# Attention on one core: row statistics of the two key sets meet by copies between partition quarters on GpSimd instead of a trip through DRAM, and q's band copy is made some steps later

## The chip, the cores and the metric

The kernel runs on one core of a Trainium2 chip. The metric is the device time of one execution in microseconds, and the median of several executions counts. On a core, TensorE (PE in the profile; its weight loads are PEld), VectorE (DVE), ScalarE (ACT), GpSimd (POOL) and SyncE (SP) each work through a queue of their own, in order. They wait for each other and for DMAs through semaphores. In this kernel SyncE issues all DMAs.

## The reference

One layer of an encoder is computed for 256 prompt tokens and 1024 sample tokens, all in float32: a feed-forward block, a mixer, a second feed-forward block, with norms around each. The mixer is dilated attention (8 heads of 64) beside a depthwise convolution. Each query attends in three dilated branches, and the branches are merged by their softmax denominators:

```python
DILATED_BRANCHES = ((128, 1), (512, 4), (2048, 16))
def dilated_attention(q, k, v):
    ...
    for window, dilation in DILATED_BRANCHES:
        o, lse = dilated_branch(q, k, v, slopes, dilation, window // (2 * dilation))
        ...
    w = jax.nn.softmax(jnp.stack(lses), axis=0)
    o = jnp.sum(w[..., None] * jnp.stack(outs), axis=0)
```

## The kernel before

The program runs its stages one after the other: feed-forward 1, the projections to q, k, v with the convolution, the attention, the output projection, feed-forward 2. Products are made of a rounded and a rest part, in three passes of TensorE (lines 198 to 200). The change touches only the attention (`attn`, line 774).

**Two key sets.** The three branches of a sample token are computed as two sets of keys. Tokens lie by residue: token 4i + c is row i of residue c. Set A holds the keys of the same residue (256 of them), set B the near keys of all residues. For set A the 256 rows of a residue are two units of 128 partitions, so a head has units 0 to 7. For set B the queries are taken in 8 bands of 128 (32 rows of each of the 4 residues), units 10 to 17, from a reordered copy `qb` of q. Units 8 and 9 are the prompt. Two units make a group, so a head has nine groups, 0 to 8.

**Statistics.** For each unit, DVE adds the bias to the scores and keeps the row minimum (line 855), and ACT takes the exponential and keeps the row sum (line 861). Both go to `st`, 128 partitions by 36 columns: column 2u is the minimum of unit u, 2u + 1 its sum. A token has one pair from set A and one from set B, in different partitions: with row i = 32 (4h + r) + j, set A has it in partition 32r + j, set B in partition 32c + j. To scale the two outputs to one softmax, the pairs must meet. This is the merge.

**The merge before.** `merge1` (line 874) transposes `st` on PE, copies it out on ACT, stores it to DRAM (`sd`) and loads it back as four pieces into `az`, where both sets stand in one order. `merge2` takes the common minimum on DVE, `merge3` the exponentials on ACT, `merge4` forms the two factors on DVE, stores them to DRAM (`fd`) and loads them broadcast over 64 partitions (`F`, the tile x in the profile). `combine1` (line 1005) multiplies the two outputs by the factors on GpSimd, for two heads at a time, and `combine2` adds them (GpSimd and DVE).

**Other work that the change touches.** `load_qk` loads q and k of the head after next into one of two sets of buffers, and before the change also makes `qb` on GpSimd (line 803). `next_tab` halves the bias tables for the next head, `tab[0]` on DVE after group 4 and `tab[1]` on GpSimd after group 8 (line 822); groups 5 to 8 of the next head read `tab[1]`.

**Order.** The code walks over 72 steps (8 heads by 9 groups): scores of this step's group, transposes of the group four steps back, products with v six steps back. `when(k, g, f)` calls f(h) k steps after group g of head h:

```python
            when(2, 8, merge1)
            when(7, 8, merge3)
            ...
            when(6, 8, merge2)
            when(8, 8, merge4)
            when(13, 8, combine2)
            ...
            when(10, 8, combine1)
```

This is not yet the order on the engines. A scheduler takes the instructions of the whole program and lays down each engine's queue by times of its own, so an instruction can stand some places earlier or later than the code has it. The order on each engine is then fixed.

Of the kernel before, what the change touches and what calls it, by code (L numbers as in the profile page):

```python
# [10 lines left out]
F32 = mybir.dt.float32  # L11
F32R = mybir.dt.float32r
AF = mybir.ActivationFunctionType
OP = mybir.AluOpType
# [3 lines left out]
P = 128  # L18
# [4 lines left out]
NS = 1024  # L23
# [5 lines left out]
NH = 8  # L29
# [119 lines left out]
class Trunk:  # L149
# [624 lines left out]
    def attn(self, qk, pool, rpool, qd, kd, vd, after):  # L774
        nc = self.nc
        mm = nc.tensor.matmul
        H = {}

        KW = 288
        bufs = []  # L780
        for i in range(2):
            q = qk[i].tile([P, NT], F32R, name=f"q{i}")
# [12 lines left out]
        def load_qk(h):  # L795
            d = H.setdefault(h, {})
            q, qb, k, d["v"] = bufs[h % 2]
            f = slice(h * HD, (h + 1) * HD)
            for i in range(2):
                nc.sync.dma_start(q[i * HD:(i + 1) * HD].bitcast(F32), qd[i, f, :])  # L800
            for z, o, s in ((0, 0, 0), (0, HD, 0), (1, 0, 1), (1, HD, 1)):
                nc.sync.dma_start(k[z][o:o + HD, :, 16:16 + 256].bitcast(F32), kd[s, f, :].rearrange("f (c i) -> f c i", c=5))
            nc.gpsimd.tensor_copy(qb.rearrange("p (b c j) -> p b c j", b=8, c=4),
                                  q[:, 0:NS].rearrange("p (c b j) -> p b c j", b=8, c=4).bitcast(F32))
            d["q"], d["qb"], d["k"] = q, qb, k

        def load_v(h):
            o = h % 2 * HD
# [62 lines left out]
                nc.vector.tensor_scalar(d["P"][u], d["P"][u], d["st"][:, 2 * u + 1:2 * u + 2], None, op0=OP.mult)  # L871


        def merge1(h):
            d = H[h]
            st = d["st"]
            ps = self.bank("psm")
            nc.tensor.transpose(ps[:36, :P], st, self.ident)
            sb = pool.tile([36, P], F32, name="asb", tag="asb", bufs=2)
            nc.scalar.activation(sb, ps[:36, :P], AF.Copy)  # L880
            sd = self.dp.tile([36, P], F32, name=f"sd{h}")
            nc.sync.dma_start(sd, sb)
            z = pool.tile([32, 4, 32], F32, name="az", tag="az", bufs=2)
            for i in range(2):
                nc.sync.dma_start(z[:, i, :], sd[0:16, :].rearrange("(c h s) (r j) -> s c h r j", h=2, s=2, j=32)[i])
                nc.sync.dma_start(z[:, 2 + i, :], sd[20:36, :].rearrange("(b s) (c j) -> s c b j", s=2, j=32)[i])
            d["z"] = z

        def merge2(h):
            d = H[h]  # L890
            z = d["z"]
            y = pool.tile([32, 4, 32], F32, name="ay", tag="ay", bufs=2)
            v = nc.vector
            v.tensor_tensor(y[:, 3, :], z[:, 0, :], z[:, 2, :], op=OP.min)
            for i in range(2):
                v.tensor_tensor(y[:, i, :], y[:, 3, :], z[:, 2 * i, :], op=OP.subtract)
            d["y"] = y

        def merge3(h):
            nc.scalar.activation(H[h]["y"][:, 0:2, :], H[h]["y"][:, 0:2, :], AF.Exp)  # L900

        def merge4(h):
            d = H[h]
            y, z, v = d["y"], d["z"], nc.vector
            for i in range(2):
                v.tensor_tensor(z[:, 2 * i + 1, :], z[:, 2 * i + 1, :], y[:, i, :], op=OP.mult)
            v.tensor_tensor(y[:, 3, :], z[:, 1, :], z[:, 3, :], op=OP.add)
            v.reciprocal(y[:, 2, :], y[:, 3, :])
            for i in range(2):
                v.tensor_tensor(y[:, i, :], y[:, i, :], y[:, 2, :], op=OP.mult)  # L910
            fd = self.dp.tile([2, NS], F32, name=f"fd{h}")
# [112 lines left out]
        load_v(0)  # L1024
        load_qk(1)
        load_v(1)

        def at(i):
# [279 lines left out]
```

## Time and profile before

| | us |
|---|---|
| median of 3 runs | 2394.32 |
| lowest, highest | 2393.75, 2397.75 |
| the profiled execution | 2392.03 |
| its span in the trace | 2390.2 |

The page gives busy time by engine for the whole span. The attention is a short part of it, from about 1203 us (first score instruction) to about 1390 us, so what matters is read from the same views limited to that stretch. Idle time of an engine counts where PE idles with it.

### The profile page before, as it was taken

To read this page: it belongs to the slowest core of one execution; us is meant where nothing else is said; L and a number is where in the kernel's file an instruction comes from. 1 tells how busy PE (TensorE), PEld (TensorE's weight loads), DVE (VectorE), ACT (ScalarE), POOL (GpSimd) and SP (SyncE) were. 2 spreads that over 40 slices of the span, in tenths; PEclk is the share of its full clock that TensorE was granted. 3 is DMA by queue.
4 is the path that set the end of the run, shared out by engine and by line. 5 is a ranking of instruction groups with operands and counts; after the bars stand their busy time and mean duration, and the time that the engine had idled before them with its cause. 6 is when DMAs were issued, how large, how long until landed. Compare 5 with 4: busy or idle time off the path is not lost.

```text
span 2390.2 us, 30540 instructions
## 1 busy us (share of the span) xinstructions
PE 2298.5 (96%) x11788; PEld 1965.1 (82%) x11788; DVE 1269.1 (53%) x1796; ACT 810.6 (34%) x1530; POOL 643.1 (27%) x574
## 2 busy tenths in 40 slices
PE   7999999999999999999978889999999999999996
PEld 6888888888788887888877778888888888788885
DVE  5743444434545576996355643743444434545557
ACT  4322222223212134654366632322222222312123
POOL 2332322321000044985112333222323223000004
PEclk9999999999999999999988999999999999999998
DMA  4212212124222343322286542212122122422224
GB/s 156 64 62 69 74 59 81 63 69 146 93 84 81 99 130 111 113 80 75 92 167 139 124 151 89 73 58 82 62 69 75 58 82 73 144 90 84 93 79 152
DMA packets 210840, 223.79 MB, mean 94 GB/s; under 512 B 32324, under 2 KB 162660, under 8 KB 210694
## 3 DMA queue, kind: packets, MB, share of 16 engines
q1 hardware_dynamic: 210694, 221.84, 30.7%
q8 instruction: 92, 1.51, 0.3%
q14 instruction: 54, 0.44, 0.1%
HBM read 163.65 MB, written 58.15 MB: 93 GB/s over the span
## 4 chain that ended last, share of the span: by engine, by line
PE 85%; DMA 5%; DVE 3%; issue 2%; ACT 2%; POOL 1%; SPq 1%; POOLq 0%; ACTq 0%; DVEq 0%
PE psAB L198 8%; PE psAB L199 8%; PE psAB L200 8%; PE psd L198 7%; PE psd L199 7%; PE psd L200 7%; PE psR L199 3%; PE psR L200 3%; PE psR L198 3%; PE psC L198 3%; PE psC L199 3%; PE psC L200 3%; PE psgu L198 2%; PE psgu L199 2%; PE psgu L200 2%
## 5 line engine op out<-in xcount | busy, mean ns | idle before, releaser
L115 DVE TENSOR_TENSOR wb<-raw,wb 128x512 fp32r<-128x512 f32 x240 | 167.2, 698 | 217.5 <-ACT wb L114 212.8
L114 ACT ACTIVATE wb<-raw 128x512 fp32r<-128x512 f32 x240 | 150.8, 629 | 329.2 <-PE psAB L200 138.4
L207 POOL TENSOR_SCALAR st<-st 128x1 f32<-128x1 f32 x70 | 40.8, 583 | 634.0 <-ACT tmp L206 361.1
L198 PE MATMUL psd<-wd,ahl 128*128 128x512 f32 x500 | 196.6, 393 | 8.9 <-ACT y L563 3.8
L199 PE MATMUL psd<-wd,ahl 128*128 128x512 f32 x500 | 194.7, 389 | 0.0
L200 PE MATMUL psd<-wd,ahl 128*128 128x512 f32 x500 | 194.7, 389 | 0.0
L452 POOL TENSOR_TENSOR ac<-ac,tmp 128x512 f32<-128x512 f32 x40 | 67.5, 1688 | 468.4 <-DVE tmp L448 445.3
L534 ACT ACTIVATE ahl<-ar 128x512 fp32r<-128x512 f32 (+1 forms) x132 | 73.0, 557 | 350.4 <-PE psd L200 251.9
L199 PE MATMUL psR<-hT2l,wb 128*128 128x256 f32 x640 | 181.1, 283 | 0.0
L200 PE MATMUL psR<-hT2h,wb 128*128 128x256 f32 x640 | 180.9, 283 | 0.0
L198 PE MATMUL psR<-hT2h,wb 128*128 128x256 f32 x640 | 180.5, 282 | 0.0
L198 PEld LDWEIGHTS psR<-hT2h,wb 128*128 128x128 f32 x640 | 122.2, 191 | 6.1
L199 PEld LDWEIGHTS psR<-hT2l,wb 128*128 128x128 f32 x640 | 122.2, 191 | 4.7
L198 PE MATMUL psAB<-hT0h,wb 128*128 128x512 f32 x320 | 125.7, 393 | 0.0
L198 PE MATMUL psC<-hT1h,wb 128*128 128x512 f32 x320 | 125.5, 392 | 0.0
L199 PE MATMUL psAB<-hT0l,wb 128*128 128x512 f32 x320 | 125.4, 392 | 0.0
L114 ACT ACTIVATE wb<-g 128x512 fp32r<-128x512 f32 x80 | 50.6, 632 | 220.8 <-POOL g L136 96.5
L199 PE MATMUL psC<-hT1l,wb 128*128 128x512 f32 x320 | 125.4, 392 | 0.0
L200 PE MATMUL psAB<-hT0h,wb 128*128 128x512 f32 x320 | 124.5, 389 | 0.0
L200 PE MATMUL psC<-hT1h,wb 128*128 128x512 f32 x320 | 124.5, 389 | 0.0
L200 PEld LDWEIGHTS psR<-hT2h,wb 128*128 128x128 f32 x640 | 122.2, 191 | 1.6
L565 DVE TENSOR_TENSOR y<-y,psd 128x1024 f32<-128x1024 f32 x70 | 85.3, 1218 | 71.2 <-PE psd L200 71.2
(385 smaller groups left out, 6263.3 us busy)
## 6 DMA issues: line engine op xcount, KB each, us to landing
raw<-in_ffn_w_gu_dram SPq DMA_DIRECT2D x88, 512.0 KB
ad<-ac SPq DMA_DIRECT2D x88, 256.0 KB
g<-in_ffn_w_down_dram SPq DMA_DIRECT2D x44, 512.0 KB
ar<-ad SPq DMA_DIRECT2D x88, 256.0 KB
raw<-in_w_in_dram SPq DMA_DIRECT2D x20, 512.0 KB
ar<-ad SPq DMA_DIRECT2D x44, 128.0 KB
ad<-x SPq DMA_DIRECT2D x40, 128.0 KB
x2d<-y SPq DMA_DIRECT2D x10, 512.0 KB
```

Of the source, the lines that this page charges most:

```text
L114: nc.scalar.activation(out[:, 0], src, AF.Copy)
L115: nc.vector.tensor_tensor(out[:, 1], src, out[:, 0].bitcast(F32), op=OP.subtract)
L198: mm(out, lh[0], rh[0], start=first, stop=False, skip_group_check=more)
L199: mm(out, lh[0], rh[1], start=False, stop=False, skip_group_check=more)
L200: mm(out, lh[1], rh[0], start=False, stop=last, skip_group_check=more)
L207: nc.gpsimd.tensor_scalar(st[:, 0:1], st[:, 0:1], 1e-6 / (mul * mul), None, op0=OP.add)
L452: nc.gpsimd.tensor_tensor(a1, a1, q, op=OP.mult)
L534: nc.scalar.activation(hl[0], r, AF.Copy)
L565: nc.vector.tensor_tensor(y[b], y[b], o, op=OP.add)
```

## The change

The first part of the merge no longer goes through DRAM. `merge1` is now 16 small copies on GpSimd: for each residue c and each quarter r, 32 partitions of set A's statistics go from partitions 32r to 32r + 31 to partitions 32c to 32c + 31, into a tile X that is laid out as set B's statistics are. `merge2` to `merge4` compute on 128 partitions by 8 columns instead of 32 by 32. The transpose on PE and the copy on ACT move behind the factors (`merge5`), where 16 columns are transposed instead of 36; the factors are then stored to `fd` by two DMAs and loaded broadcast as before. The steps of the merge are called at other distances. The copy `qb` of the head after next is called eight steps after group 8 instead of with the loads, and at the start for heads 0 and 1.

```diff
@@ load_qk
-            nc.gpsimd.tensor_copy(qb.rearrange("p (b c j) -> p b c j", b=8, c=4),
-                                  q[:, 0:NS].rearrange("p (c b j) -> p b c j", b=8, c=4).bitcast(F32))
+        def cast_qb(h):
+            q, qb = bufs[h % 2][0:2]
+            nc.gpsimd.tensor_copy(qb.rearrange("p (b c j) -> p b c j", b=8, c=4),
+                                  q[:, 0:NS].rearrange("p (c b j) -> p b c j", b=8, c=4).bitcast(F32))
@@ merge1
-            nc.tensor.transpose(ps[:36, :P], st, self.ident)
...
-            nc.sync.dma_start(sd, sb)
...
-                nc.sync.dma_start(z[:, i, :], sd[0:16, :].rearrange("(c h s) (r j) -> s c h r j", h=2, s=2, j=32)[i])
-                nc.sync.dma_start(z[:, 2 + i, :], sd[20:36, :].rearrange("(b s) (c j) -> s c b j", s=2, j=32)[i])
+            d["X"] = pool.tile([P, 8, 2], F32, name="ax", tag="ax", bufs=2)
+            x = d["X"].rearrange("p (h r) s -> p h r s", h=2)
+            for c in range(4):
+                for r in range(4):
+                    nc.gpsimd.tensor_copy(x[c * 32:(c + 1) * 32, :, r, :],
+                                          d["st"][r * 32:(r + 1) * 32, 4 * c:4 * c + 4].rearrange("p (h s) -> p h s", s=2))
@@ merge2
-            v.tensor_tensor(y[:, 3, :], z[:, 0, :], z[:, 2, :], op=OP.min)
+            v(y[:, 3], d["X"][:, :, 0], z[:, :, 0], op=OP.min)
...
@@ merge4, merge5
-            nc.sync.dma_start(fd.rearrange("s (p j) -> p s j", j=32), y[:, 0:2, :])
+        def merge5(h):
+            ps = self.bank("psm")
+            nc.tensor.transpose(ps[:16, :P], d["y"].rearrange("p i b -> p (i b)")[:, 0:16], self.ident)
+            sb = pool.tile([16, P], F32, name="asb", tag="asb", bufs=2)
+            nc.scalar.activation(sb, ps[:16, :P], AF.Copy)
+            for i in range(2):
+                nc.sync.dma_start(fd[i].rearrange("(c b j) -> b c j", c=4, b=8), sb[8 * i:8 * i + 8].rearrange("b (c j) -> b c j", c=4))
@@ the steps
-            when(2, 8, merge1)
-            when(7, 8, merge3)
+            when(5, 8, merge5)
+            when(3, 8, merge3)
...
-            when(6, 8, merge2)
-            when(8, 8, merge4)
+            when(1, 8, merge1)
+            when(2, 8, merge2)
+            when(4, 8, merge4)
+            when(8, 8, lambda h: cast_qb(h + 2) if h + 2 < NH else None)
```

Up to the attention the queues are the same. In it, three places show what the change moves. Lines of the changed kernel are some numbers higher: the score instruction is 858, the q copy 807, the table 825, the first product of `combine1` 1013.

DVE, merge of head 1, before: it stands behind the scores of group 3 of head 2 (L855 is a score instruction, L894 and L896 are `merge2`, `az` is loaded from DRAM).

```order
L855 ISA pr,ast<-pss,g 128x256
L855 ISA ast 128x1
L894 TENSOR_TENSOR ay<-az 32x32
L896 TENSOR_TENSOR ay<-ay,az 32x32 x2
L855 ISA pr,ast<-pss,g 128x256
L855 ISA ast 128x1
L855 ISA pr,ast<-pss,g 128x256
L855 ISA ast 128x1
L924 COPY pT<-pst 128x512
```

DVE, merge of head 1, now: L892 to L894 are `merge2`, `ax` is the tile that GpSimd's copies fill, `ast` holds the statistics.

```order
L858 ISA pr,ast<-pss,g 128x256
L858 ISA ast 128x1
L929 COPY pT<-pst 128x512
L892 TENSOR_TENSOR ay<-ax,ast 128x8
L893 TENSOR_TENSOR ay<-ay,ax 128x8
L894 TENSOR_TENSOR ay<-ay,ast 128x8
L858 ISA pr,ast<-pss,g 128x256
L858 ISA ast 128x1
L858 ISA pr,ast<-pss,g 128x256
L858 ISA ast 128x1
L902 TENSOR_TENSOR ay<-ax,ay 128x8
```

The merge stands right behind the scores of group 8 of its own head, four groups earlier, and it waits for GpSimd where it waited for a DMA.

POOL before, from the q copy for head 3 on: L803 is the q copy, L822 the table, L1008 and L1017 are `combine1` and `combine2` of heads 0 and 1.

```order
L803 CAST qb1_9269<-q1_9268 128x1024
L822 TENSOR_SCALAR g_9279<-g_9279 128x768
L803 CAST qb0_9259<-q0_9258 128x1024
L822 TENSOR_SCALAR g_9279<-g_9279 128x768
L1008 TENSOR_TENSOR to_9707<-to_9707,x_9653 128x1024
L1008 TENSOR_TENSOR to_9706<-to_9706,x_9654 128x1024
L1017 TENSOR_TENSOR hT0h_9218<-to_9706,to_9707 128x512
L1017 TENSOR_TENSOR hT1h_9220<-to_9706,to_9707 128x512
L803 CAST qb1_9269<-q1_9268 128x1024
```

POOL now, from the table after head 1 to the copies of head 3: L884 are the 16 copies, `ax_9954` is head 2's and `ax_10200` head 3's.

```order
L825 TENSOR_SCALAR g_9279<-g_9279 128x768
L807 CAST qb1_9269<-q1_9268 128x1024
L884 COPY ax_9954<-ast_9705 32x2x2 x16
L1013 TENSOR_TENSOR to_9734<-to_9734,x_9585 128x1024
L1013 TENSOR_TENSOR to_9733<-to_9733,x_9586 128x1024
L825 TENSOR_SCALAR g_9279<-g_9279 128x768
L807 CAST qb0_9259<-q0_9258 128x1024
L1022 TENSOR_TENSOR hT0h_9218<-to_9733,to_9734 128x512
L1022 TENSOR_TENSOR hT1h_9220<-to_9733,to_9734 128x512
L884 COPY ax_10200<-ast_9945 32x2x2 x16
```

Each head's 16 copies have come into the queue. The products of heads 0 and 1 (L1013) now stand ahead of the table after head 2 and of the q copy for head 4, where they stood behind both.

SP before, merge of head 2: L882 and L885, L886 are the trip through `sd`, L912 stores `fd`; L800, L802, L812 and L814 load q, k and v.

```order
L882 DMA sd2_9950<-asb_9948 36x128
L812 DMA v0_9262<-vd_88 128x2x64
L885 DMA az_9952<-sd2_9950 32x1x32
L886 DMA az_9952<-sd2_9950 32x1x32
L885 DMA az_9952<-sd2_9950 32x1x32
L886 DMA az_9952<-sd2_9950 32x1x32
L800 DMA q1_9268<-qd_86 64x1280 x2
L814 DMA v0_9262<-vd_88 32x9x64 x4
L812 DMA v1_9272<-vd_88 128x2x64 x3
L802 DMA kH1_9270<-kd_87 64x5x256 x2
L912 DMA fd2_10115<-ay_10054 32x2x32
L802 DMA kL1_9271<-kd_87 64x5x256 x2
```

SP now, merge of head 2: L917 stores `fd` in two DMAs, L924 loads it broadcast; L800, L802, L815 and L817 load q, k and v.

```order
L817 DMA v0_9262<-vd_88 32x9x64
L917 DMA fd2_10068<-asb_10066 8x4x32 x2
L817 DMA v0_9262<-vd_88 32x9x64
L924 DMA x_10071<-fd2_10068 64x1024
L924 DMA x_10072<-fd2_10068 64x1024
L817 DMA v0_9262<-vd_88 32x9x64 x2
L800 DMA q1_9268<-qd_86 64x1280 x2
L815 DMA v1_9272<-vd_88 128x2x64 x4
L802 DMA kH1_9270<-kd_87 64x5x256 x2
```

The five DMAs through `sd` and `az` are gone; the store of the factors is two DMAs, and the loads of q for head 5 stand behind the broadcast loads.

## Rows read from the trace of the kernel before

**Rows 1.** The page of the profiled execution: its span, and part 1, the busy time of each engine with its share of the span and its instructions.

```profile
span 2390.2 us, 30540 instructions
...
PE 2298.5 (96%) x11788; PEld 1965.1 (82%) x11788; DVE 1269.1 (53%) x1796; ACT 810.6 (34%) x1530; POOL 643.1 (27%) x574
```

**Rows 2.** Stretches of the span, five of the attention: the stretch in us, its length, then busy time and count of instructions of PE, PEld, DVE, ACT and POOL, the granted TensorE clock (1.00 is full), the busy share of the DMA engines and GB/s.

```profile
1240.00:1376.00 136.00, 113.06 (x675) 100.43 (x675) 76.63 (x331) 86.04 (x278) 38.47 (x22) 0.88 0.62 132
1262.00:1274.00 12.00, 11.86 (x85) 10.84 (x84) 6.28 (x27) 8.53 (x30) 9.57 (x6) 1.00 0.87 174
1274.00:1279.30 5.30, 1.16 (x9) 0.91 (x8) 1.33 (x8) 0.99 (x4) 0.78 (x1) 0.91 0.09 14
1279.30:1286.00 6.70, 6.70 (x26) 5.90 (x27) 5.68 (x21) 3.87 (x14) 0.00 (x0) 0.56 0.75 153
1286.00:1298.00 12.00, 11.48 (x82) 10.30 (x81) 6.97 (x30) 9.19 (x31) 3.14 (x2) 1.00 0.87 178
```

**Rows 3.** Who waited for whom between 1200 and 1410 us, all engines: total us, times, longest us.

```profile
DVE ay L894 <- DMA az<-sd: 37.3, 8, 5.8
...
PE pst L930 <- DVE ast L855: 20.2, 6, 4.4
```

**Rows 4.** The chain that ended last, between 1265 and 1282 us, in order of time: start us, us, what. SPq is the queue of SyncE, which issues the DMAs.

```profile
1268.26 6.86 DMA sd<-asb
...
1275.14 0.73 SPq L885
...
1275.92 1.92 DMA az<-sd
...
1279.27 1.08 PE pst L930 x4
```

**Rows 5.** Timeline of DVE, start us, us, what (in brackets the idle time before it and what ended it). L855 is the score instruction, two to a group, nine groups to a head: the first of head 1; of group 7 of head 2 and group 3 of head 3; of group 7 of head 3 and group 3 of head 4; of head 7, and of its groups 3 and 7, with the merge between these two.

```profile
1219.39 0.42 DVE L855 CUSTOM_DVE_ANT_0 pr<-pss,g 128x256 f32<-128x256 f32 x1 [2.26 <-PE pss L851]
...
1262.21 0.43 DVE L855 CUSTOM_DVE_ANT_0 pr<-pss,g 128x256 f32<-128x256 f32 x1 [2.24 <-PE pss L851]
...
1271.62 0.42 DVE L855 CUSTOM_DVE_ANT_0 pr<-pss,g 128x256 f32<-128x256 f32 x1
...
1285.88 0.42 DVE L855 CUSTOM_DVE_ANT_0 pr<-pss,g 128x256 f32<-128x256 f32 x1 [1.01 <-PE pss L851]
...
1295.91 0.42 DVE L855 CUSTOM_DVE_ANT_0 pr<-pss,g 128x256 f32<-128x256 f32 x1
...
1357.73 0.42 DVE L855 CUSTOM_DVE_ANT_0 pr<-pss,g 128x256 f32<-128x256 f32 x1 [0.61 <-PE pss L851]
...
1363.70 0.42 DVE L855 CUSTOM_DVE_ANT_0 pr<-pss,g 128x256 f32<-128x256 f32 x1
...
1366.35 0.18 DVE L894 TENSOR_TENSOR ay<-az 32x32 f32<-32x32 f32 x1 [1.86 <-DMA az<-sd]
...
1373.00 0.35 DVE L855 CUSTOM_DVE_ANT_0 pr<-pss,g 128x256 f32<-128x256 f32 x1
```

**Rows 6.** Timelines of DVE (the merge in head 3) and of PE right behind it.

```profile
1277.94 0.18 DVE L894 TENSOR_TENSOR ay<-az 32x32 f32<-32x32 f32 x1 [5.54 <-DMA az<-sd]
...
1279.27 1.08 PE L930 MATMUL pst<-ident,pr 128*128 128x128 f32 x4 [4.14 <-DVE ast L855]
```

**Rows 7.** Groups of instructions between 1200 and 1410 us on POOL: line, engine, operation, names, shapes, count | busy us, mean ns | idle time before.

```profile
L822 POOL TENSOR_SCALAR g<-g 128x768 f32<-128x768 f32 x7 | 15.0, 2137 | 26.9 <-DVE ast L855 24.2 <-DVE ay L910 2.7
L1008 POOL TENSOR_TENSOR tmp<-tmp,x 128x1024 f32<-128x1024 f32 x4 | 9.5, 2383 | 31.6 <-DMA x<-fd 30.6 <-ACT asb L880 1.1
...
L803 POOL CAST qb<-q 128x1024 fp32r<-128x1024 f32 x7 | 7.3, 1044 | 91.4 <-DMA fd<-ay 40.2 <-DMA q<-qd 27.3 <-PE pss L851 23.9
L1017 POOL TENSOR_TENSOR hT0h<-tmp 128x512 fp32r<-128x512 f32 x2 | 2.6, 1285 | 0.2
```

**Rows 8.** The smallest instructions of POOL in the whole span, by source line: count, then ns least/median/most, first and last start.

```profile
L207 POOL TENSOR_SCALAR st<-st x70: 214/223/1317, 5.5 to 2384.4; 128x1 f32<-128x1 f32 x70
...
L605 POOL MEMSET glu<- x4: 111/112/117, 902.3 to 1039.0; 128x15 f32 x4
```

**Rows 9.** Timelines of POOL and DVE at two places, start us, us: a cast beside two merge instructions, and a one-element instruction beside a DVE instruction with two inputs.

```profile
1236.56 1.04 POOL L803 CAST qb<-q 128x1024 fp32r<-128x1024 f32 x1 [9.15 <-DMA q<-qd]
...
1236.67 0.96 DVE L896 TENSOR_TENSOR ay<-ay,az 32x32 f32<-32x32 f32 x1
...
1416.41 1.28 DVE L212 SCALAR_TENSOR_TENSOR tmp<-x,st,g 128x1024 f32<-128x1024 f32 x1 [4.67 <-ACT tmp L206]
...
1416.49 1.27 POOL L207 TENSOR_SCALAR st<-st 128x1 f32<-128x1 f32 x1
```

**Rows 10.** Timelines of SyncE's queue (start us, us of an issue) and of POOL: the store and the two broadcast loads with which the merge of head 1 ends, the issue of q that stands behind the loads of the next merge, and the product that uses the broadcast rows.

```profile
1262.21 0.41 SPq L912 DMA_DIRECT2D fd<-ay  x1
...
1263.81 1.09 SPq L919 DMA_DIRECT2D x<-fd  x2
...
1278.06 1.15 SPq L800 DMA_DIRECT2D q<-qd  x2
...
1267.48 4.70 POOL L1008 TENSOR_TENSOR to<-to,x 128x1024 f32<-128x1024 f32 x2 [0.61 <-ACT asb L880]
```

**Rows 11.** The tail: timeline of SyncE's queue and of PE where the last weights of the output projection come.

```profile
1395.44 2.12 SPq L77 DMA_DIRECT2D raw<-in_w_out_dram  x1
...
1405.04 0.50 PE L198 MATMUL pso<-whi,hT2h 128*128 128x512 f32 x1 [1.87 <-ACT whi L90]
```

More of the change, by code (lines that the diff above doesn't have):

```diff
@@ L802, in load_qk @@
                 nc.sync.dma_start(k[z][o:o + HD, :, 16:16 + 256].bitcast(F32), kd[s, f, :].rearrange("f (c i) -> f c i", c=5))
+            d["q"], d["qb"], d["k"] = q, qb, k
+        def cast_qb(h):
+            q, qb = bufs[h % 2][0:2]
             nc.gpsimd.tensor_copy(qb.rearrange("p (b c j) -> p b c j", b=8, c=4),
                                   q[:, 0:NS].rearrange("p (c b j) -> p b c j", b=8, c=4).bitcast(F32))
-            d["q"], d["qb"], d["k"] = q, qb, k
         def load_v(h):
@@ L875, in merge1 @@
             d = H[h]
-            st = d["st"]
-            ps = self.bank("psm")
-            nc.tensor.transpose(ps[:36, :P], st, self.ident)
-            sb = pool.tile([36, P], F32, name="asb", tag="asb", bufs=2)
-            nc.scalar.activation(sb, ps[:36, :P], AF.Copy)
-            sd = self.dp.tile([36, P], F32, name=f"sd{h}")
-            nc.sync.dma_start(sd, sb)
-            z = pool.tile([32, 4, 32], F32, name="az", tag="az", bufs=2)
-            for i in range(2):
-                nc.sync.dma_start(z[:, i, :], sd[0:16, :].rearrange("(c h s) (r j) -> s c h r j", h=2, s=2, j=32)[i])
-                nc.sync.dma_start(z[:, 2 + i, :], sd[20:36, :].rearrange("(b s) (c j) -> s c b j", s=2, j=32)[i])
@@ L887, in merge1 @@
-            d["z"] = z
+            d["X"] = pool.tile([P, 8, 2], F32, name="ax", tag="ax", bufs=2)
[4 more added lines that the diff above has]
+                                          d["st"][r * 32:(r + 1) * 32, 4 * c:4 * c + 4].rearrange("p (h s) -> p h s", s=2))
         def merge2(h):
             d = H[h]
-            z = d["z"]
@@ L892, in merge2 @@
-            y = pool.tile([32, 4, 32], F32, name="ay", tag="ay", bufs=2)
-            v = nc.vector
-            v.tensor_tensor(y[:, 3, :], z[:, 0, :], z[:, 2, :], op=OP.min)
-            for i in range(2):
-                v.tensor_tensor(y[:, i, :], y[:, 3, :], z[:, 2 * i, :], op=OP.subtract)
-            d["y"] = y
+            y = d["y"] = pool.tile([P, 4, 8], F32, name="ay", tag="ay", bufs=2)
+            z = d["B"] = d["st"][:, 20:36].rearrange("p (b s) -> p b s", s=2)
+            v = nc.vector.tensor_tensor
@@ L899, in merge3 @@
+            v(y[:, 3], d["X"][:, :, 0], z[:, :, 0], op=OP.min)
+            v(y[:, 0], y[:, 3], d["X"][:, :, 0], op=OP.subtract)
+            v(y[:, 1], y[:, 3], z[:, :, 0], op=OP.subtract)
         def merge3(h):
-            nc.scalar.activation(H[h]["y"][:, 0:2, :], H[h]["y"][:, 0:2, :], AF.Exp)
+            nc.scalar.activation(H[h]["y"][:, 0:2], H[h]["y"][:, 0:2], AF.Exp)
         def merge4(h):
             d = H[h]
-            y, z, v = d["y"], d["z"], nc.vector
-            for i in range(2):
-                v.tensor_tensor(z[:, 2 * i + 1, :], z[:, 2 * i + 1, :], y[:, i, :], op=OP.mult)
@@ L907, in merge4 @@
-            v.tensor_tensor(y[:, 3, :], z[:, 1, :], z[:, 3, :], op=OP.add)
-            v.reciprocal(y[:, 2, :], y[:, 3, :])
+            y, v = d["y"], nc.vector.tensor_tensor
+            v(y[:, 2], d["X"][:, :, 1], y[:, 0], op=OP.mult)
+            v(y[:, 3], d["B"][:, :, 1], y[:, 1], op=OP.mult)
+            v(y[:, 3], y[:, 2], y[:, 3], op=OP.add)
+            nc.vector.reciprocal(y[:, 2], y[:, 3])
+            for i in range(2):
+                v(y[:, i], y[:, i], y[:, 2], op=OP.mult)
+        def merge5(h):
+            d = H[h]
+            ps = self.bank("psm")
+            nc.tensor.transpose(ps[:16, :P], d["y"].rearrange("p i b -> p (i b)")[:, 0:16], self.ident)
+            sb = pool.tile([16, P], F32, name="asb", tag="asb", bufs=2)
+            nc.scalar.activation(sb, ps[:16, :P], AF.Copy)
+            fd = self.dp.tile([2, NS], F32, name=f"fd{h}")
@@ L909, in merge4 @@
             for i in range(2):
-                v.tensor_tensor(y[:, i, :], y[:, i, :], y[:, 2, :], op=OP.mult)
-            fd = self.dp.tile([2, NS], F32, name=f"fd{h}")
-            nc.sync.dma_start(fd.rearrange("s (p j) -> p s j", j=32), y[:, 0:2, :])
+                nc.sync.dma_start(fd[i].rearrange("(c b j) -> b c j", c=4, b=8), sb[8 * i:8 * i + 8].rearrange("b (c j) -> b c j", c=4))
             if h % 2 == 0:
@@ L1026, in attn @@
         load_v(1)
+        cast_qb(0)
+        cast_qb(1)
         def at(i):
```

## The prediction

> **What bounds the kernel now.** Over the whole span TensorE is the bound: PE is busy for 96% of it [rows 1]. So I first looked for the place where it is not. In the stretches of the attention PE is idle for 22.9 of 136 us, and the granted clock is 0.88 of full on average [rows 2]. One head shows the rhythm: 12 us with PE busy for 11.86 at full clock, then 5.3 us with PE busy for 1.16, then 6.7 us with PE busy all the time at a granted clock of 0.56, near the lower level of 1.2 GHz. It is the same work as before, done more slowly. The idle time has one cause. In the list of waits DVE's first merge instruction waits 37.3 us in eight times for the loads of `az`, and PE's transposes wait 20.2 us in six times for DVE [rows 3]. The chain gives the parts of one such wait: the store to `sd` takes 6.86 us from its issue until the loads can go, the load 1.92 us [rows 4]. DVE works in order, so the scores of the next groups stand behind the merge, and PE runs dry. A DVE wait of 5.54 us shows as a PE idle time of 4.14 us [rows 6]; 1.40 us are absorbed by work that PE has ahead.
>
> **What the change removes.** The merge no longer waits for DRAM on DVE. I size the gain by the pace of groups that wait for no merge. Five groups (7 of one head to 3 of the next) take 9.41 us and 10.03 us at two places, 9.72 on average. The other four (3 to 7) are shortest in head 7: 9.30 us, of which 1.86 is its merge's wait, so 7.44 [rows 5]. A head without merge wait is 9.72 + 7.44 = 17.16 us. From the first score of head 1 to that of head 7 now takes 138.34 us; six heads at 17.16 are 102.96, so 35.4 less. Head 7's wait adds 1.86 - 1.40 = 0.5: **35.9 us gross**. Another way comes out close: PE's 20.2 us of waiting, and 0.12 of 136 us lost to the clock, 16.3, are 36.5. I take it that without the gaps the clock stays at full, as in the 12 us stretches [rows 2].
>
> What is late next is PE itself: in the 12 us stretch it has no idle time left. The DMAs come near behind it. They are busy for 0.62 of 136 us, 84 us of work, which in 103 us is 0.82; the 12 us stretch ran at 0.87 [rows 2], so the loads of q, k and v fit.
>
> **What the change adds.** *The copies.* No row shows a copy between quarters. The nearest are one-element POOL instructions, 0.214 us at least and 1.317 at most, and a memset of 15 elements at 0.111 [rows 8]. I take 0.214, since a copy of four elements per partition is nearest to it; 16 are 3.4 us a head. POOL's other work is 2.14 + 1.04 and, for two heads, 2 x 2.38 + 2 x 1.28 = 7.3, so 6.8 a head [rows 7]. Together 10.3 of 17.2 us: hidden, since set A's statistics are complete after group 3 and the merge stands behind group 8.
>
> *DVE's instructions.* Nine before, nine now, smaller: nothing. The transpose, ACT's copy and exponentials remain, one of each: nothing. SP issues four DMAs for a merge instead of eight. `fd` still has to land before the broadcast loads go, with the next q behind them; q is needed most of a head later: nothing.
>
> *The q copy.* It moves back by eight steps; what it writes is first read in group 5 of the head after next, and in its old place it made POOL wait for loads [rows 7]. Behind it on POOL now stand `combine2` or the next head's copies. I charge nothing here, and the risk below.
>
> *The new place of the merge.* It stands where POOL is busiest: the table (2.14 us) becomes ready at the same moment, and after every second head the two products (4.77 us) fall there. DVE and POOL hold each other up: a merge instruction with two inputs took 0.96 us beside a POOL cast of 1.04 and ended as it ended, while its like takes 0.18, and a one-element POOL instruction took 1.27 us beside a DVE instruction with two inputs [rows 6, 9]. The new merge reads two tiles from SBUF in eight of nine instructions. After heads 0, 1, 3 and 5 a hold can be one table, 2.14 - 1.40 = 0.74 us each, 3.0; after heads 2, 4 and 6 two products, 4.77 - 1.40 = 3.4 each, 10.1. So 0 to 13.1 us; below nothing is excluded, since a hold can only delay. I take **6**, somewhat under the middle, because DVE can get in between two POOL instructions. The Trainium skill (GPSIMD Engine Reference, section 8, Key points) says that GpSimd shares its SBUF interfaces with VectorE and contends with DVE instructions of two SBUF inputs. The trace agrees with 0.96 against 0.18 us; by that rule the term is there, without it the forecast would be 6 us lower.
>
> *The products ahead of the table.* DVE's `combine2` part (line 1023 now) stands behind group 3 and waits for POOL's, which now stands behind products, table and q copy. I take **2** for three such places; the rival below has the other end.
>
> *The tail.* The last weights of the output projection are issued behind the merge of head 7, and PE idles 1.87 us for them [rows 11]. With a shorter merge this shrinks by 0 to 1.9: I take **1** off.
>
> Net: 35.9 - 6 - 2 + 1 = 28.9 us. The profiled execution took 2392.0, so 2363.1; the median lies 2.3 above it, so **2365 us**.
>
> **The rivals.** *The wait moves to `combine2`.* In the trace the products start 3.67 us after the issue of their broadcast loads [rows 10]. Then follow 4.77 (products), 2.14 (table), 1.04 (q copy) and 1.28 (first sum): 12.9 us after the issue. If the loads are issued as late against the groups as now, 1.6 us after the score of group 7, the score of group 3 comes 7.8 us after them [rows 5, 10] and DVE waits about 5.1 us, PE 3.7; with 2.7 for the clock (16.3 over six gaps) 6.4 a time, 19 for three. 35.9 - 19 - 6 + 1 = 12: 2382 us. Against it: the merge starts four groups earlier, so the loads should, too; for it: four POOL instructions in a row that used to stand the other way round. 13%.
>
> *Slow copies.* If a copy whose input and output lie in different quarters ran at a quarter of the pace, it would take 4 x 0.214 = 0.86 us, POOL 13.7 + 6.8 = 20.5 us a head, and POOL would set the pace: 6 x 20.5 = 123, 15 us less than now, and 13 less with the other terms: 2381 us. No row excludes it. 8%. The Trainium skill has such a rule (same page and section): only two of the eight cores of GpSimd reach all partitions, and a kernel that needs the full reach runs at 25% of the engine; no run so far shows whether it holds for copies between quarters.
>
> *Slower than before.* POOL as the bound again, but with each copy at the most that a row shows, 1.317 us: 21.1 + 6.8 = 27.9 us a head, 167 us for six against 138, and some 2423 us in all. It decides from (138.3 / 6 - 6.8) / 16 = 1.0 us per copy. For it: a held one-element instruction took 1.27 us [rows 9]; against it: of 70 such the median is 0.223 [rows 8], and DVE's scores read one input from PSUM. 4%.
>
> *No change.* The loads take the place of the wait: q, k, v and the factors keep their pace of 84 us of work in 136, because their issues wait for each other. Against it: 0.87 busy in the good stretches, and q was itself held by the merge (its issue at 1278.06 stands behind the `az` loads, rows 10). 5%, at 2394 us.
>
> **How the numbers follow.** The forecast has 70%, with a range of its own from 2354 (no hold, and all of 36.5 with some 4 of head 1) to 2376 (holds at 13, `combine2` waiting a little). The others have 13, 8, 5 and 4%. The range of 8 in 10 takes in the forecast and the two rivals at 2381 and 2382 in good part: 2354 to 2382. A measurement of this kernel can tell about 0.2%, 4.8 us, from no change. Faster by more: 70 + 13 + 8 = 91%. Within: 5%. Slower: 4%.
>
> **What would show it.** In the profile after: DVE's merge (L892) waits for POOL for well under 1 us; the idle time of PE before the transposes falls from 20 to a few us; the granted clock stays at 1.00 through the attention; the scores of one head follow those of the last by 17 to 18 us; a copy takes about 0.2 us. Merge instructions of 1 to 2 us beside the table and the products would show the holds; a long wait of L1023 for POOL the first rival; copies of 0.8 us or more the second and third. A DMA wait in front of scores would make the forecast wrong in a way that I have not priced beyond no change.

## The result, and the profile after

The changed kernel takes **2359.62 us**, median of four runs (2355.94 to 2363.50), against 2394.54 (2393.75 to 2397.75, four runs): ratio 0.9852, 95% interval 0.9833 to 0.9871, 34.9 us less. The profiled execution is the slowest of the four, 2363.50 us; against that of before (2392.0) it is 28.5 less. Its page, span and part 1:

```profile
span 2361.7 us, 30596 instructions
...
PE 2287.1 (97%) x11788; PEld 1958.5 (83%) x11788; DVE 1277.8 (54%) x1796; ACT 809.4 (34%) x1530; POOL 674.1 (29%) x702
```

PE's busy time fell by 11.4 us, the span by 28.5 [rows 1]: what went is mostly waiting, and some work at a low clock. POOL has 128 instructions more, the copies.

Stretches (length, busy time of PE, PEld, DVE, ACT and POOL with counts, granted clock, DMA share, GB/s): from the first score of head 1 to that of head 7, then 8 us in head 2, two times 8 us in head 3, and 8 us at the start of head 7:

```profile
1219.00:1332.00 113.00, 102.67 (x689) 93.59 (x687) 83.97 (x327) 83.42 (x275) 58.05 (x118) 0.97 0.93 182
1240.00:1248.00 8.00, 8.00 (x58) 7.47 (x57) 5.36 (x22) 7.02 (x23) 4.58 (x17) 1.00 1.14 197
1256.00:1264.00 8.00, 6.00 (x42) 5.33 (x40) 1.29 (x8) 3.03 (x11) 8.00 (x5) 1.00 1.10 206
1264.00:1272.00 8.00, 4.87 (x18) 4.42 (x19) 7.35 (x20) 4.35 (x14) 6.56 (x18) 0.60 0.79 158
1332.00:1340.00 8.00, 6.87 (x36) 6.40 (x37) 5.17 (x26) 4.99 (x18) 6.39 (x13) 0.79 0.08 31
```

Head 2 is as wanted: PE busy for all of 8.00 us at full clock. Head 3 is not: a gap, and then 4.87 of 8 us busy at a granted clock of 0.60, between the two levels of 1.2 and 2.4 GHz, right behind it. That is the pattern of before [rows 2], once in full instead of in every head; a weaker one (0.79) follows the losses at the end of head 6. From the first score of head 1 to that of head 7, PE's idle time fell from 24.9 us (113.48 busy of 138.34 before) to 10.3, and its busy time by 10.8 us, with the granted clock at 0.97 instead of 0.88.

The first score of heads 1 to 7 (timeline of DVE; L858 is now the score line):

```profile
1219.35 0.42 DVE L858 CUSTOM_DVE_ANT_0 pr<-pss,g 128x256 f32<-128x256 f32 x1 [1.60 <-PE pss L854]
...
1235.35 0.42 DVE L858 CUSTOM_DVE_ANT_0 pr<-pss,g 128x256 f32<-128x256 f32 x1
...
1251.57 0.42 DVE L858 CUSTOM_DVE_ANT_0 pr<-pss,g 128x256 f32<-128x256 f32 x1 [0.26 <-PE pss L854]
...
1275.33 0.42 DVE L858 CUSTOM_DVE_ANT_0 pr<-pss,g 128x256 f32<-128x256 f32 x1
...
1294.68 0.41 DVE L858 CUSTOM_DVE_ANT_0 pr<-pss,g 128x256 f32<-128x256 f32 x1
...
1311.28 0.42 DVE L858 CUSTOM_DVE_ANT_0 pr<-pss,g 128x256 f32<-128x256 f32 x1
...
1332.27 0.41 DVE L858 CUSTOM_DVE_ANT_0 pr<-pss,g 128x256 f32<-128x256 f32 x1
```

The differences are 16.00, 16.22, **23.76**, **19.35**, 16.60 and **20.99**, in all 112.92 against 138.34 [rows 5]: 25.4 us less. Heads 1, 2 and 5 are undisturbed, heads 3, 4 and 6 lose 15.3 us against the mean of these three (16.27). Who waited for whom from 1200 to 1360 us (total, times, longest):

```profile
DVE to L1023 <- POOL hT0h L1022: 6.8, 1, 6.8
...
PE pss L853 <- DVE ast L858: 5.1, 1, 5.1
...
PE pst L935 <- ACT pr L864: 1.2, 3, 0.9
```

The merge waits for no DMA any more, and `az` and `sd` are gone from the list. PE waited 20.2 us for DVE in front of the transposes [rows 3]; now it waits 0.3 us for DVE there, and 1.2 us in three times for ACT (2.4 before). What is left is one wait of `combine2` (L1023) for POOL, with 5.1 us of PE behind it. The chain that ended last shows how it came about (start, us, what):

```profile
1245.22 6.28 DMA fd<-asb
...
1251.51 3.93 DMA x<-fd
...
1255.61 1.13 POOL to L1013
...
1260.31 0.46 POOL g L825
...
1262.34 1.05 POOL qb L807
1263.39 1.24 POOL hT0h L1022
...
1264.65 1.73 DVE to L1023
...
1267.13 0.58 PE pss L853
```

Head 1's factors: the stores (1245.22) need 6.28 us until the loads can go, the loads 3.93; the two products start at 1255.61, and behind them POOL makes the table (L825), the copy of q (L807) and the first sum (L1022). Only then can DVE go on, and the scores of group 4 stand behind it. Some 7.6 us had gone before the stores: DVE finished the factors at 1237.63, PE, busy throughout, transposed them at 1242.02, ACT copied them out at 1242.86, and SP's queue came to the first store at 1245.22.

The other two losses, heads 4 and 6, are merge instructions beside POOL's products (L1013). Timelines of POOL and DVE after heads 4 and 6; the last three rows are the table (L825) and two merge instructions after head 1:

```profile
1292.29 2.37 POOL L1013 TENSOR_TENSOR tmp<-tmp,x 128x1024 f32<-128x1024 f32 x1 [7.54 <-issue]
...
1292.42 2.26 DVE L893 TENSOR_TENSOR ay<-ay,ax 128x8 f32<-128x8 f32 x1
...
1295.36 1.64 DVE L902 TENSOR_TENSOR ay<-ax,ay 128x8 f32<-128x8 f32 x1
...
1327.58 2.37 POOL L1013 TENSOR_TENSOR to<-to,x 128x1024 f32<-128x1024 f32 x1 [5.74 <-issue]
...
1327.65 2.32 DVE L892 TENSOR_TENSOR ay<-ax,ast 128x8 f32<-128x8 f32 x1
1330.01 2.26 DVE L893 TENSOR_TENSOR ay<-ay,ax 128x8 f32<-128x8 f32 x1
...
1234.29 2.14 POOL L825 TENSOR_SCALAR g<-g 128x768 f32<-128x768 f32 x1 [4.54 <-DVE ast L858]
...
1234.65 0.48 DVE L892 TENSOR_TENSOR ay<-ax,ast 128x8 f32<-128x8 f32 x1
...
1235.17 0.17 DVE L893 TENSOR_TENSOR ay<-ay,ax 128x8 f32<-128x8 f32 x1
```

A merge instruction of 128x8 takes 2.26 us beside a product (the one at 1292.42 ends at 1294.68, the product at 1294.66). One instruction gets in between two products, the next waits again. Beside the table the hold is short: the one that starts 0.36 us into it takes 0.48 us and ends 0.84 us after the table's start, the next takes 0.17.

The copies, by group (count | busy us, mean ns | idle before):

```profile
L884 POOL COPY ax<-ast 32x4 f32<-32x4 f32 x128 | 31.2, 244 | 13.7 <-ACT pr L864 8.9
```

By source line the least is 177 ns, the median 182, the most 984. The 31.2 us are 3.9 a head.

The rest of the gain lies behind head 7's first score. The 56 us that follow it, first of the kernel before, then of this one:

```profile
1357.70:1413.70 56.00, 48.88 (x251) 40.36 (x250) 30.04 (x80) 27.20 (x64) 18.22 (x12) 0.97 0.50 153
```

```profile
1332.30:1388.30 56.00, 52.52 (x261) 44.40 (x262) 32.06 (x80) 29.38 (x68) 21.88 (x30) 0.94 0.46 138
```

PE is busy for 3.6 us more of them; its wait of 1.87 us for the last weights [rows 11] is gone. From the first score of head 7 to the end it is 3.1 us less than before.

### The profile page after: what moved, and what is told of

Read it like the earlier page. It is cut to its first block, busy times and chain, and to the rows that moved or that the text cites. A ratio compares the mean times of both kernels' runs of the same rounds, so it can differ in the third digit from the quotient of the medians.

```text
span 2361.7 us, 30596 instructions
## 1 busy us (share of the span) xinstructions
PE 2287.1 (97%) x11788; PEld 1958.5 (83%) x11788; DVE 1277.8 (54%) x1796; ACT 809.4 (34%) x1530; POOL 674.1 (29%) x702
## 4 chain that ended last, share of the span: by engine, by line
PE 88%; DVE 3%; DMA 3%; issue 2%; ACT 2%; POOL 2%; SPq 0%; POOLq 0%; ACTq 0%; DVEq 0%
PE psAB L198 8%; PE psAB L199 8%; PE psAB L200 8%; PE psd L198 7%; PE psd L199 7%; PE psd L200 7%; PE psR L199 3%; PE psR L200 3%; PE psR L198 3%; PE psC L198 3%; PE psC L199 3%; PE psC L200 3%; PE psgu L198 2%; PE psgu L199 2%; PE psgu L200 2%
```

## Experiments

Three groups of four runs, each group beside the kernel before on its own chip (2395.2 to 2395.6 us there). A difference of under 4 us between two medians of four or five runs is not told apart from none here: executions of the changed kernel spread over 7.6 us. The changed kernel was run again beside the third group only (run 10). Each run's profile is of one execution.

**1. The later copy of q alone** (`cast_only`), on the kernel before:

```diff
+        cast_qb(0)
+        cast_qb(1)
...
+            when(8, 8, lambda h: cast_qb(h + 2) if h + 2 < NH else None)
```

> The kernel before with q's band copy alone made eight steps later; the merge keeps its trip through DRAM. Theory (the gain is the merge's): the same as before, 2394 within 5 us, and DVE still waits 30 us or more in all for the loads of az. Rival (the copy of q held POOL and with it the loads, so its new place brings a part of the gain): 2385 or less.

Measured 2394.92 us (10 runs), ratio 0.9997 (0.9986 to 1.0007). The merge still waits for its loads, from 1200 to 1410 us:

```profile
DVE ay L897 <- DMA az<-sd: 37.4, 8, 6.2
```

**2. The merge alone** (`merge_only`), the changed kernel without that part:

```diff
-        cast_qb(0)
-        cast_qb(1)
...
-            when(8, 8, lambda h: cast_qb(h + 2) if h + 2 < NH else None)
```

> The changed kernel with q's band copy back at its old place. Theory (the gain is the merge's): the changed kernel's time, 2360 within 5 us. Rival (the later copy is a part of the gain): 2366 or more, and POOL's copies of the merge or the products wait for loads of q.

Measured 2360.91 us (2358.07 to 2364.16). Runs 1 and 2 together: the gain is the merge's, and the moved copy of q is worth nothing that can be measured.

**3. DRAM kept, DVE's part later** (`dram_after7`). Is it DVE's place in line that cost, or the trip?

```diff
+            if h + 1 < NH:
+                v.tensor_copy(y[:, 3, 0:1], H[h + 1]["st"][0:32, 28:29])
...
-            when(7, 8, merge3)
+            when(10, 8, merge3)
...
-            when(6, 8, merge2)
-            when(8, 8, merge4)
-            when(13, 8, combine2)
+            when(9, 8, merge2)
+            when(11, 8, merge4)
+            when(16, 8, combine2)
...
-            when(10, 8, combine1)
+            when(13, 8, combine1)
```

> The kernel before, its trip through DRAM kept with all eight transfers, but the DVE part of the merge held back until group 7 of the next head has its scores (a one-element copy that reads that group's statistics stands ahead of it), and what follows moved with it. Theory (the cost was that DVE stood in order behind a wait for DRAM, with the scores of the next groups behind it; not the transfers themselves): DVE's waits for az under 8 us in all, against 37; and at least two thirds of the gain, 2360 to 2372 us. Rival (the transfers and SP's queue were the cost): 2385 us or more.

Measured 2379.45 us (2377.46 to 2382.81), 16 less than before: neither number. DVE's wait for `az` is down to 5.8 us in two times, 2.3 of it in heads 1 to 6, as the theory has it, but DVE now waits 7.2 and 7.1 us for POOL's `combine2`, behind group 8 of heads 3 and 5:

```profile
1282.40 1.73 DVE L1020 TENSOR_TENSOR to<-to 128x512 f32<-128x512 f32 x1 [7.19 <-POOL hT0h L1019]
```

**4. The same with `combine2` called later too** (`dram_late2`), against run 3:

```diff
+                    if h < 7:
+                        nc.gpsimd.tensor_copy(hi[:, 0:1], H[h + 2]["st"][:, 28:29])
...
-            when(16, 8, combine2)
+            when(18, 8, lambda h: combine2(h) if h < 7 else None)
+            when(16, 8, lambda h: combine2(h) if h == 7 else None)
```

> The kernel before with its trip through DRAM, the DVE part of the merge behind group 7 of the next head as in the earlier run, and now combine2 of heads 1, 3 and 5 four to five groups later too, so that DVE stands behind neither trip. Theory (the trips cost only through DVE's order): 2358 to 2366 us, as the changed kernel, without any copy on POOL. Rival (the eight transfers and SP's queue cost by themselves, by late loads): 2372 us or more.

Measured 2382.17 us (2380.80 to 2383.69): on the rival's side, but the edit did not do what it was meant to. DVE's `combine2` stands behind group 8 of heads 3 and 5 as it did in run 3, and waits 7.2 and 7.9 us there (at 1282.72, against 1282.40 in run 3). So DVE still stands behind the second trip, and the question stays unanswered. One wait, then the timelines of SP's queue, POOL and DVE that lead to it:

```profile
DVE to L1022 <- POOL hT0h L1021: 7.2, 1, 7.2
```

```profile
1263.19 0.41 SPq L914 DMA_DIRECT2D fd<-ay  x1
1263.69 0.34 SPq L882 DMA_DIRECT2D sd<-asb  x1
...
1269.49 0.72 SPq L885 DMA_DIRECT2D az<-sd  x1
...
1272.37 1.15 SPq L921 DMA_DIRECT2D x<-fd  x2
...
1276.55 2.36 POOL L1010 TENSOR_TENSOR to<-to,x 128x1024 f32<-128x1024 f32 x1 [13.37 <-ACT tmp L974]
...
1282.72 1.73 DVE L1022 TENSOR_TENSOR to<-to 128x512 f32<-128x512 f32 x1 [7.20 <-POOL hT0h L1021]
```

Two trips in a row are too long. The stores of `fd` and `sd` go out at 1263.19 and 1263.69, the loads of `az` stand behind them in SP's queue until `sd` has landed (1269.49), and the loads of `fd` behind those (1272.37), 9.2 us after their store. The products start at 1276.55 and DVE waits 7.2 us. Heads 2, 4 and 6, which hold no such wait, take 18.44, 15.64 and 16.20 us (19.52, 15.89 and 17.52 in run 3), against 25.06, 21.98 and 22.83 before and 16.00 to 16.60 of the changed kernel's undisturbed heads. Head 1 stays at 21.25 (21.36 in run 3): DVE waits 4.0 us (2.3) for `az` there even behind group 7. Heads 3 and 5 take 26.42 and 28.50. So DVE's place in line made most of the wait in heads 2, 4 and 6, and the length of the trip is paid at `combine2` when the merge is moved back. Part of that is the experiment's own, since its merge ends later and its `fd` meets the next merge's `az`. Whether the transfers cost anything when DVE stands behind neither trip is not shown.

**5. The copies twice** (`copies_twice`):

```diff
+            x2 = pool.tile([P, 8, 2], F32, name="ax2", tag="ax2", bufs=2).rearrange("p (h r) s -> p h r s", h=2)
...
+                for r in range(4):
+                    nc.gpsimd.tensor_copy(x2[c * 32:(c + 1) * 32, :, r, :],
+                                          d["st"][r * 32:(r + 1) * 32, 4 * c:4 * c + 4].rearrange("p (h s) -> p h s", s=2))
```

> The changed kernel with each of the 16 copies between quarters made twice, the second time into a tile that nothing reads: 16 x 0.18 = 2.9 us more on POOL per head, 23 us in all. Theory (POOL's copies are hidden): 2360 within 3 us. Rival (POOL's time is on the path of the merge or of the products behind it): 2366 or more, up to 2380 if all of it counts; DVE's L1023 then waits longer for POOL than 6.8 us.

Measured 2359.47 us (2355.68 to 2369.19), the changed kernel's time in the median; one of the four runs took 9 us more than the next. POOL's groups (count | busy us, mean ns | idle before):

```profile
L888 POOL COPY ax<-ast 32x4 f32<-32x4 f32 x128 | 30.5, 238 | 5.2
L885 POOL COPY ax<-ast 32x4 f32<-32x4 f32 x128 | 27.5, 215 | 10.8 <-ACT pr L864 5.9
```

Some 27 us more on POOL cost nothing that can be measured: the copies are hidden with room to spare.

**6. Products in pieces** (`pieces`), against the holds:

```diff
-                    nc.gpsimd.tensor_tensor(t, t, f, op=OP.mult)
+                    for c in range(0, NS, 256):
+                        nc.gpsimd.tensor_tensor(t[:, c:c + 256], t[:, c:c + 256], f[:, c:c + 256], op=OP.mult)
```

> The changed kernel with each of POOL's products, 1024 columns at 2.3 us each, cut into four of 256 columns. Theory (the 8 us that the merge instructions take too long after heads 4 and 6 are DVE held for the length of a whole POOL instruction): no merge instruction takes over 0.8 us, heads 4 and 6 lose under 2 us each against 3.75 and 5.92, and the time falls by 2 to 6 us. Rival (DVE is held for as long as POOL has such work queued, whatever the size of a piece, or the losses of these heads are something else): long instructions stay or heads 4 and 6 stay at 19 us or more, the time within 2 us or longer by the fixed cost of the pieces.

After head 4, timelines of POOL and DVE:

```profile
1288.47 2.11 POOL L1014 TENSOR_TENSOR tmp<-tmp,x 128x256 f32<-128x256 f32 x3 [5.39 <-issue]
...
1289.95 0.66 DVE L893 TENSOR_TENSOR ay<-ay,ax 128x8 f32<-128x8 f32 x1
...
1291.29 0.70 DVE L902 TENSOR_TENSOR ay<-ax,ay 128x8 f32<-128x8 f32 x1
```

The holds shrank with the piece: 0.66 and 0.70 us, a piece being 0.74 on average. Heads 4 and 6 took 17.78 and 16.48 us in this execution, the fastest of the four. The mechanism is shown; the time, 2358.56 us (2353.33 to 2360.79), is not told apart from the changed kernel's, because head 3 still lost 5.5 us and the runs spread.

**7. The store of `fd` from ACT's queue** (`fd_act`):

```diff
-                nc.sync.dma_start(fd[i].rearrange("(c b j) -> b c j", c=4, b=8), sb[8 * i:8 * i + 8].rearrange("b (c j) -> b c j", c=4))
+                nc.scalar.dma_start(fd[i].rearrange("(c b j) -> b c j", c=4, b=8), sb[8 * i:8 * i + 8].rearrange("b (c j) -> b c j", c=4))
```

> The changed kernel with the stores of fd issued from ACT's queue, not SP's, where loads of q and k stand ahead. Theory (the factors land late because their store and loads share SP's queue with large loads: 6.3 us from store to load, 3.9 more to the products): store to load falls to 3 us or less, the products start 2 to 4 us earlier and the wait of 6.8 us shrinks by as much, 2 to 4 us off. Rival (the DMAs' own time, or ACT's issue of two DMAs of some tenths of a us each in front of its exponentials): within 1 us, or slower by up to 3 us.

Timelines of ACT, SP, POOL and DVE:

```profile
1232.51 0.51 ACT L864 ACTIVATE pr<-pr,ast 128x256 f32<-128x256 f32 x1 [5.94 <-DMA fd<-asb]
...
1247.33 0.66 ACTq L917 DMA_DIRECT2D fd<-asb  x2
...
1249.89 1.10 SPq L924 DMA_DIRECT2D x<-fd  x2
...
1253.89 2.37 POOL L1013 TENSOR_TENSOR to<-to,x 128x1024 f32<-128x1024 f32 x1 [6.42 <-DMA x<-fd]
...
1254.94 1.35 DVE L892 TENSOR_TENSOR ay<-ax,ast 128x8 f32<-128x8 f32 x1
1256.32 2.26 DVE L893 TENSOR_TENSOR ay<-ay,ax 128x8 f32<-128x8 f32 x1
```

For head 1's factors it is 2.56 us now from store (1247.33) to loads (1249.89) instead of 6.28, and no wait of L1023 is left in heads 1 to 6. Over all eight heads the gain is smaller: 2.62 us on average against 3.50, and heads 0 (3.77) and 2 (4.17) are about where they were (3.37 and 4.62). But in head 1 ACT's exponentials stood 5.94 us behind the store, and the earlier products now meet the merge of head 2: 1.35 and 2.26 us, each ending with a product. The time is 2357.53 us (2353.44 to 2360.83), within the noise of no change. In heads 1 to 6 of this execution the losses trade against each other: 112.82 us, against 112.92.

**8. `combine2`'s sums on DVE** (`sum_on_dve`):

```diff
-                    nc.gpsimd.tensor_tensor(hi, ta[:, c], tb[:, c], op=OP.add)
-                    nc.vector.tensor_tensor(ta[:, c], ta[:, c], tb[:, c], op=OP.add)
-                    nc.vector.tensor_tensor(lo, ta[:, c], hi.bitcast(F32), op=OP.subtract)
+                    s = d["F"][0]
+                    nc.vector.tensor_tensor(s[:, c], ta[:, c], tb[:, c], op=OP.add)
+                    nc.vector.tensor_copy(hi, s[:, c])
+                    nc.vector.tensor_tensor(lo, s[:, c], hi.bitcast(F32), op=OP.subtract)
```

> The changed kernel with the rounded sum of combine2 on DVE too (sum into one of the factor tiles, a copy that rounds, the rest), so that DVE waits for POOL's two products alone and no longer for the table, q's copy and a first sum that stand behind them on POOL. Theory (the wait of 6.8 us in head 3 is POOL's queue behind the products): the wait shrinks to under 3 us, and the time falls by 3 to 6 us against the changed kernel, less about 1 us for three more DVE instructions of some 0.5 us in each of four heads. Rival (the wait is the factors' late landing): the wait stays above 5 us and the time stays or grows by up to 3 us.

Measured 2365.63 us (2364.19 to 2365.94), 6 more than the changed kernel, and a wait that grew:

```profile
DVE x L1023 <- POOL to L1013: 11.1, 2, 6.4
```

The question isn't answered by it. With no step on POOL in between, the program's scheduler put the sums some groups earlier on DVE: behind group 0 of head 3, from which it then took 9.12 us to group 1, and behind group 1 of head 5 (7.46 us). What it shows is only that the products are not ready at these earlier places.

**9. Both 6 and 8** (`sum_pieces`), the edits as above:

> The changed kernel with both: combine2's sums on DVE, and the products in pieces of 256 columns. Theory (two separate losses, the wait of combine2 and the holds of the merge): both go, every head at 16 to 17.5 us, 5 to 12 us off, 2348 to 2355 us. Rival (the losses trade against each other, since the attention's other engines then stand next): under 3 us off the better of the two alone.

Measured 2368.81 us (2367.08 to 2372.09): worse than either; from group 0 of head 3 to group 1 it took 10.31 us, the place where run 8 lost 9.12.

**10. The changed kernel again** (`after_again`), beside the next two and run 4:

> The changed kernel unedited, for a comparison on the same chip with the three beside it: 2360 within 3 us.

Measured 2359.07 us (2356.57 to 2361.58). In this profiled execution, 2356.57 us, heads 1 to 6 take 108.30 us, 4.6 less than in the one shown above; the longest wait of L1023 is 5.0 us, and heads 3, 4 and 6 take 21.16, 19.43 and 18.86.

**11. `combine2` behind group 7** (`late`), on the changed kernel, with the two added lines of `combine2` from run 4 and

```diff
-            when(13, 8, combine2)
+            when(18, 8, lambda h: combine2(h) if h < 7 else None)
+            when(13, 8, lambda h: combine2(h) if h == 7 else None)
```

> The changed kernel with combine2 of heads 1, 3 and 5 behind group 7 of the head after next instead of group 3 (a one-element POOL copy that reads that group's statistics stands ahead of each first sum). Theory (what is left of head 3's loss is DVE standing in order behind products whose factors land late; given four more groups it waits for nothing): no wait of L1025 for POOL over 1 us in the seven heads, head 3 at 17 us or less against 23.8, and 3 to 6 us off. Rival (the wait is only moved, to POOL or to the tiles that are freed later): another wait of 3 us or more, the time within 2 us.

Measured 2356.12 us (2352.27 to 2363.47): not told apart from 2359.07. The wait of `combine2` for POOL is 1.0 us at most, but heads 3 and 5 stay long in the profiled execution, the slowest of the five (18.85 and 22.04): DVE now does `combine2` and the merge in one place, and in head 5 it waits 3.0 us for the table, which POOL makes behind the products. Head 6 (19.21) still has the holds, 1.97 and 2.27 us.

**12. Run 11 with the pieces of run 6** (`late_pieces`):

> The same, and the products in pieces of 256 columns. Theory (wait and holds are the two losses that are left): every head from 1 to 6 within 16 to 17.5 us, from the first score of head 1 to that of head 7 some 99 to 103 us against 112.9, PE's clock at 1.00 throughout, 6 to 10 us off: 2350 to 2354 us. Rival (loads or PE's other feeders are next): the heads stay at 17.5 us or more on average and the gain is under 3 us.

Measured **2352.73 us** (2352.26 to 2353.23), ratio to the kernel before 0.9823 (0.9809 to 0.9837). All four runs lie below all four of the changed kernel beside it, 6.3 us between the medians. It is not told apart from run 11 (3.4 us), whose five runs spread over 11. From the first score of head 1 to that of head 7 it is 105.76 us, more than the 99 to 103 expected: heads 3 and 5 still take 19.62 and 21.38 us, the other four 15.58 to 16.96. The stretch of heads 1 to 6, and the longest wait of DVE for POOL in it:

```profile
1217.00:1325.00 108.00, 101.82 (x691) 92.28 (x692) 81.58 (x334) 84.28 (x280) 60.31 (x139) 1.00 0.97 189
```

```profile
DVE pr L858 <- POOL g L825: 2.0, 1, 2.0
```

The clock stays at 1.00, and PE is busy for 101.8 of 108 us. The DMA engines' share is 0.97, but that is not shown to be a bound: single stretches of 8 us above show up to 1.14, and PE's only wait for a load here is 1.7 us. Of the 4.3 us between this profiled execution and that of run 10, 1.4 lie ahead of the attention's first score, where nothing was changed.

## Why the prediction was right

The time, 2365 us in a range from 2354 to 2382, came out at 2359.62. The mechanism was the forecast one, and the net term, 28.9 us, is nearly what the profiled execution shows (28.5). That it is so near is luck, since two parts of the sum were missed by over 5 us each and cancelled:

- **The gross gain was sized too low.** A head without waits takes 16.00, 16.22 and 16.60 us, on average 16.27, not 17.16. Six heads at that pace are 40.7 us less than before, not 35.4. The 17.16 were put together from groups of heads that hold a merge [rows 5], 9.72 and 7.44 us; in the changed kernel, from head 1 to head 3, the same groups take about 9.0 and 7.2. Head 0 of the kernel before, which holds no merge, takes 16.61 us and would have been the nearer measure.
- **The holds were sized well in sum, wrongly in place.** The forecast had 6 us. Heads 4 and 6, with the products beside the merge, are 3.1 and 4.7 us longer than 16.27, 7.8 in all. Of this 1.8 and 3.9 us stand at the holds themselves, from group 8 to the next head's first score (3.75 and 5.92 us, against 1.99 in head 2); where the rest comes from is not shown. At head 6 that is more than the 3.4 allowed for a place, as two merge instructions were held there, one by each product. The table, for which up to 3.0 were allowed, cost next to nothing: it held a merge instruction for 0.3 us at most. Run 6 shows the cause of the holds.
- **The first rival came true at one place of three.** The forecast charged 2 us; DVE's wait of 6.8 us (the rival said 5.1) made head 3 7.5 us longer than 16.27, and the other two places waited 0.2 us or not at all. The chain was that of the rival: products, table, copy of q, first sum. Its condition was late loads, and the argument against it, that the loads come earlier because the merge does, failed here: they went 3.4 us after the score of group 7 (1248.13), 1.6 before [rows 5, 10]. The merge's lead was lost between the factors and the stores (7.6 us) and between the stores and the loads (6.28 us; run 7: 2.56 on another queue).
- **The tail gave 3.1 us**, not 1 and the 0.5 of head 7: 28.5 less the 25.4 of heads 1 to 6. In run 10 it gave 5.2, so its size is uncertain by some 2 us.

So 40.7 - 7.8 - 7.5 + 3.1 = 28.5: 6.9 us better than forecast in the first and last terms, 7.3 worse in the other two. The median is 5 us below the forecast because this execution is the slowest of its four, where the forecast put the median 2.3 above: in another (run 10) heads 1 to 6 take 4.6 us less, 2.6 of them in head 3 and 2.1 in head 6.

The steps charged at nothing held. *The copies* take 0.182 us in the median and 0.244 on average (forecast 0.214), 3.9 us a head instead of 3.4, and are hidden twice over (run 5), so the second rival and the slower one are out. The Trainium skill (GPSIMD Engine Reference, section 8, Key points) speaks of 25% of the engine for a kernel that needs the full reach; the trace does not show that here, since a copy between quarters takes 0.182 us in the median and a one-element instruction 0.223 [rows 8]. *The copy of q* is neutral (runs 1 and 2). *SP* was put down as nothing; whether the four transfers that went were worth something stays open. Runs 3 and 4 show loads of `fd` standing behind loads of `az` in SP's queue, but they also move `fd`.

*The main step*, that DVE stood in order behind a wait for DRAM, is borne out by the waits that went (all 37.3 us of DVE for `az`; of PE's 20.2 us for DVE 5.4 are left, 5.1 of them behind `combine2`), and by runs 3 and 4 in heads 2, 4 and 6. It is not shown to be the whole: keeping the trip and moving only DVE's place got 16 and 13 us, under half, with DVE waiting at `combine2` instead.

Of the signs, the clock at 1.00 throughout failed in head 3 (0.60) and behind head 6 (0.79), no head took the 17 to 18 us (three took 16.0 to 16.6, three 19.4 to 23.8), and the DMA share was 0.93 over heads 1 to 6 where 0.82 was reckoned; the loads fitted all the same.

## What to carry to other kernels

When an engine that works in order waits in the middle of a loop, size the gain by the parts that do not wait, and then look at the next instruction on that engine which depends on a slower one: part of the gain is lost there. A GpSimd product of 2.37 us held VectorE's two-input instructions to its end; where such an instruction can fall beside short ones on the critical path, cut it into pieces. Removing one such loss alone may show in the profile and not in the time, as in runs 6 and 11; with both removed the time moved (run 12).

## What the hardware showed that was not expected

- How long the hold lasts depends on POOL's instruction. Beside a product of 2.37 us a merge instruction takes up to 2.3 us and ends with it, beside a piece of 0.74 us 0.66 to 0.70. Beside the table of 2.14 us it is held only in the first part: in all the runs together, the 37 that start 0.03 to 0.6 us into a table end 0.84 to 0.86 us after its start, and those that start later are not held by it (0.15 to 0.18 us). That the table has one input is not the reason: the q copy has one input too, and the merge instruction beside it is held to its end (0.96 us beside 1.04 [rows 9]; 1.01 us beside 1.04 in run 10). The Trainium skill (SBUF — State Buffer, Who interferes with whom) calls it an exclusive lock for the whole instruction between a DVE instruction with two SBUF inputs and a GpSimd instruction that reads SBUF. The trace agrees for the products (run 7: 1254.94 + 1.35 is 1256.29, the product's end 1256.26) and for the q copy. For the table it agrees only in the first 0.84 us, and there the measurement decides; why the hold ends there is not shown.
- The way of 4 KB stores to their loads through DRAM varied from head to head: from the first store to the loads 1.3 to 6.3 us, 3.5 on average, on the queue that also carries the loads of q, k and v, and 1.3 to 4.2 us, 2.6 on average, with the stores on ACT's (run 7). ACT, on the other hand, once stood idle for 5.94 us around issuing them.
